# Level products of a gated linear mixer: from zero-padded queries of two heads to one product per head on 64 rows

## The chip, the cores and the metric

The kernel runs on one core of one Trainium2 chip. The metric is device time in microseconds, from launch to end; the profiled execution's span is the time from the first to the last instruction on the core. TensorE's granted clock is reported beside it as a share of its full 2.4 GHz.

## The reference: what is computed

The program is one layer of a hybrid encoder on 2048 tokens of width 1024: a normalization, a projection to 13 groups of columns, four mixers of width 256 each (S5, HGRN2, FoX attention, mLSTM), an output projection, and a SwiGLU feed-forward part, with residuals. All in float32.

The change touches the HGRN2 mixer alone. It has 4 heads of 64 channels. With gates `lf` (logarithms of decays), queries `q`, keys `k` and values `v`, one chunk computes

```
b = cumsum(lf) over time
scores[t, s] = sum over channels of q[t] * k[s] * exp(b[t] - b[s])      for s <= t, else 0
o = (q * exp(b)) @ state + scores @ v
state = exp(b_last) * state + (k * exp(b_last - b))^T @ v
```

The decay is per channel, so `exp(b[t] - b[s])` can't be pulled out of the sum as one factor per time without overflow; it has to be split at a point between s and t.

## The kernel before, in words

The 2048 tokens are handled in four blocks of 512 (`BLK`), each of four chunks of 128 (`P`). The projection of blocks 0 and 1 comes first, then that of blocks 2 and 3, then for each block the output projection and the feed-forward part. `hgrn_mix(c, b)` (L458) runs once per block: for blocks 0 and 1 it is put among the projections as work of high priority (L1660 to L1666), for blocks 2 and 3 it stands in `mixers` (L1626) beside the feed-forward part of the block before. The order in which each engine gets its instructions is not written out by hand. A planner simulates the program with its own costs, places each instruction by priority and by the time at which its operands are ready, and fixes one order per engine; buffers rotate within pools (`tile_pool`), and an instruction that takes a buffer waits for its last readers. So the dense matmuls of the projections (L279, L297) and of the feed-forward part (L1478 gate and up, L1503 down) lie between the mixer's instructions on TensorE.

Channels lie on partitions: a "head pair" p holds 128 rows, head 2p on rows 0 to 63 and head 2p+1 on rows 64 to 127; time lies along the free dimension. For the scores of a chunk, the kernel splits time in seven levels (`LEVELS`, h = 64, 32, ..., 1). At level h each window of 2h times has its keys in its first half and its queries in its second, both decayed towards the window's middle. A level product is one set of matmuls in which all windows of a chunk are done together, and a mask (`c.lvl`) picks the blocks of the result that belong to the level.

For each pair and level the loop at L499 does this:

- GpSimd subtracts the middle's `b` (L509), ScalarE takes two exponentials (L513 for keys, L514 for queries), each 128x256.
- VectorE multiplies the keys into `hK` (L516, 128x256; the halves that hold no keys are zero from a memset at L478) and the queries into `hQ` (L520). `hQ` has the shape 128 x 2 x 256: for each of the two heads a full-height operand in which the rows of the other head stay zero, from the memset at L478. So there are two half-height multiplications, one per head. At level 1 GpSimd copies the queries instead (L526), and the keys are used as they are.
- TensorE does four matmuls (L530), one per chunk: the 128x128 keys of both heads as weights, the padded queries of both heads (2 x 64 columns) as the moving operand. Because of the zeros one product over 128 rows gives both heads' scores side by side, in one PSUM tile from `c.psS` (four buffers, tag `s`, shared with the other mixers and with the transposes of L109).
- VectorE copies the masked blocks into `hA[p]` (L534, `copy_predicated`, 128x512).

After the seven levels of a pair follow the rest of its operands (L535 to L549): decayed queries and keys in place (L541, L542), and the diagonal of each chunk's last time, made with `hL` (L548) and copied into `hA` (L550). After both pairs: transposes of the keys (L567), state updates (L576, L584), outputs from the state and from `hA` (L591, L595), the head-wise normalization and the gate. The gates are loaded into buffers of the tag `hb`, which hold `b` before (L553).

A float32 matmul appears in the trace as two records, each a weight load (PEld) and a matmul (PE); here they are called passes. The dense matmuls work on operands split in two float32r parts, and each of them is one pass.

Of the kernel before, what the change touches and what calls it, by code (L numbers as in the profile page):

```python
# [8 lines left out]
F32 = mybir.dt.float32  # L9
# [3 lines left out]
AF = mybir.ActivationFunctionType  # L13
ALU = mybir.AluOpType
# [4 lines left out]
P = 128  # L19
D = 1024  # L20
KD = D // P
BLK = 512
NEG = -1e30
EPS = 1e-6
LEVELS = (64, 32, 16, 8, 4, 2, 1)
# [153 lines left out]
def l3(t):  # L179
    return t.rearrange("p (c l) -> p c l", l=P)  # L180
# [277 lines left out]
def hgrn_mix(c, b):  # L458
    nc, tc = c.nc, c.tc
    with ExitStack() as ctx:  # L460
        def tp(name, bufs):
            return ctx.enter_context(tc.tile_pool(name=name, bufs=bufs, side=c.side, reuse_waits="tile"))

        p1, p2, ptmp = tp("h_p1", 1), tp("h_p2", 2), tp("h_tmp", 4)

        def ps():
            return c.psS.tile([P, 512], F32, name="ps", tag="s")

        def tmp(name):
            return ptmp.tile([P, BLK], F32, name=name, tag="tmp")  # L470

        nk = 4
        hA = [p1.tile([P, 2, BLK], F32, name=f"hA{p}") for p in range(2)]
        hK = [p1.tile([P, BLK], F32, name=f"hK{p}") for p in range(nk)]
        hQ = [p1.tile([P, 2, 256], F32, name=f"hQ{p}") for p in range(nk)]
        hL = [p1.tile([P, 2, 4], F32, name=f"hL{p}") for p in range(2)]
        for t in (*hA, *hK, *hQ, *hL):
            nc.gpsimd.memset(t, 0.0)  # L478
        v = p1.tile([P, 4, 256], F32, name="hv")
        qs, ks, bs, qes, kds, ebs = [], [], [], [], [], []  # L480
# [9 lines left out]
        for p in range(2):  # L490
            eb = p2.tile([P, 4], F32, name="heb")
            nc.scalar.activation(eb, l3(bs[p])[:, :, P - 1], AF.Exp)
            for h in range(2):
                s = slice(64 * h, 64 * h + 64)
                nc.gpsimd.tensor_copy(hL[p][s, h], l3(qs[p])[s, :, P - 1])
            ebs.append(eb)
        for p in range(2):
            A4 = hA[p].rearrange("p h (c l) -> p h c l", l=P)
            for i, h in enumerate(LEVELS):  # L499
                w = 2 * h  # L500
                nb = BLK // w
                q3 = qs[p].rearrange("p (n w) -> p n w", w=w)
                k3 = ks[p].rearrange("p (n w) -> p n w", w=w)
                Q = hQ[(7 * p + i) % nk]
                if h > 1:
                    b3 = bs[p].rearrange("p (n w) -> p n w", w=w)
                    dd = tmp("hd")
                    d3 = dd.rearrange("p (n w) -> p n w", w=w)
                    nc.gpsimd.tensor_tensor(d3, b3, b3[:, :, h - 1:h].to_broadcast([P, nb, w]), ALU.subtract)  # L509
                    ee = tmp("he")  # L510
                    eq = ee[:, 0:256].rearrange("p (n w) -> p n w", w=h)
                    ek = ee[:, 256:512].rearrange("p (n w) -> p n w", w=h)
                    nc.scalar.activation(ek, d3[:, :, 0:h], AF.Exp, scale=-1.0)  # L513
                    nc.scalar.activation(eq, d3[:, :, h - 1:2 * h - 1], AF.Exp)  # L514
                    K = hK[(7 * p + i) % nk]
                    nc.vector.tensor_tensor(K.rearrange("p (n w) -> p n w", w=w)[:, :, 0:h],  # L516
                                            k3[:, :, 0:h], ek, ALU.mult)
                    for hh in range(2):
                        s = slice(64 * hh, 64 * hh + 64)
                        nc.vector.tensor_tensor(Q[s, hh].rearrange("p (n w) -> p n w", w=h),  # L520
                                                q3[s, :, h - 1:2 * h - 1], eq[s], ALU.mult)
                else:
                    K = ks[p]
                    for hh in range(2):
                        s = slice(64 * hh, 64 * hh + 64)
                        nc.gpsimd.tensor_copy(Q[s, hh].rearrange("p (n w) -> p n w", w=1), q3[s, :, 0:1])  # L526
                pt = ps()
                p3 = pt.rearrange("p (h t) -> p h t", h=2)
                for t in range(4):
                    nc.tensor.matmul(p3[:, :, t * 64:(t + 1) * 64], lhsT=K[:, t * P:(t + 1) * P],  # L530
                                     rhs=Q[:, :, t * 64:(t + 1) * 64], start=True, stop=True)
                av = hA[p].rearrange("p h (n w) -> p h n w", w=w)[:, :, :, h - 1:2 * h - 1]
                mv = c.lvl[:, i].rearrange("p (n w) -> p n w", w=h)[:, None].to_broadcast([P, 2, nb, h])
                nc.vector.copy_predicated(av, mv, pt.rearrange("p (h n w) -> p h n w", h=2, w=h))  # L534
            q, k, bb = qs[p], ks[p], bs[p]  # L535
            b3 = l3(bb)
            e1, e2 = tmp("he1"), tmp("he2")
            nc.gpsimd.tensor_tensor(l3(e2), b3, b3[:, :, P - 1:P].to_broadcast([P, 4, P]), ALU.subtract)
            nc.scalar.activation(e1, bb, AF.Exp)
            nc.scalar.activation(e2, e2, AF.Exp, scale=-1.0)  # L540
            nc.vector.tensor_tensor(q, e1, q, ALU.mult)  # L541
            nc.vector.tensor_tensor(k, e2, k, ALU.mult)  # L542
            qes.append(q)
            kds.append(k)
            pt = ps()
            pl = pt[:, 0:8].rearrange("p (h t) -> p h t", h=2)
            for t in range(4):
                nc.tensor.matmul(pl[:, :, t], lhsT=kds[p][:, t * P:(t + 1) * P], rhs=hL[p][:, :, t],  # L548
                                 start=True, stop=True)  # L549
            nc.vector.tensor_copy(A4[:, :, :, P - 1], pl)  # L550
        gs = []
        for u in range(2):
            g = p2.tile([P, BLK], F32, name="hgs", tag="hb").rearrange("p (t n) -> p t n", t=2)  # L553
# [8 lines left out]
        for u in range(2):  # L562
            pt = ps()
# [7 lines left out]
        for u in range(2):  # L571
            pd = ps()
            for i in range(2):
                for p in range(2):
                    cs = slice((2 * i + p) * P, (2 * i + p + 1) * P)
                    nc.tensor.matmul(pd[:, cs], lhsT=kts[u][:, cs], rhs=v[:, 2 * u + i, p * P:(p + 1) * P],  # L576
                                     start=True, stop=True)
            pd = pd.rearrange("p (i a h d) -> p i a h d", i=2, a=2, h=2)
            for i in range(2):
                t = 2 * u + i  # L580
                for p in range(2):
                    for h in range(2):
                        s = slice(64 * h, 64 * h + 64)
                        nc.vector.scalar_tensor_tensor(S[t + 1][s, p, h], S[t][s, p, h], ebs[p][s, t:t + 1],  # L584
                                                       pd[s, i, p, h], ALU.mult, ALU.add)
            po = ps()
            for i in range(2):
                t = 2 * u + i
                for p in range(2):
                    cs = slice((2 * i + p) * P, (2 * i + p + 1) * P)  # L590
                    nc.tensor.matmul(po[:, cs], lhsT=qes[p][:, t * P:(t + 1) * P],  # L591
                                     rhs=S[t][:, p].rearrange("p h d -> p (h d)"), start=True, stop=False)
                    for h in range(2):
                        c0 = (2 * i + p) * P + h * 64
                        nc.tensor.matmul(po[:, c0:c0 + 64], lhsT=hA[p][:, h, t * P:(t + 1) * P],  # L595
                                         rhs=v[:, t, p * P + h * 64:p * P + h * 64 + 64], start=False, stop=(h == 1))
            nc.scalar.activation(v[:, 2 * u:2 * u + 2], po.rearrange("p (t n) -> p t n", t=2), AF.Copy)
        f = p2.tile([P, 16], F32, name="hf")
# [393 lines left out]
def s5_mats(c, tp, s4q, kt_tile, ps, NCH):  # L992
# [121 lines left out]
    def build(gb, m):  # L1114
# [458 lines left out]
def hybrid_block(ctx, tc, x, w_in, gate_bias, s5_lambda_re, s5_lambda_im, s5_b_re, s5_b_im, s5_c_re,  # L1573
# [52 lines left out]
    def mixers(b):  # L1626
        mlstm_mix(c, b)
        fox_mix(c, b)
        if b + 1 < NB:
            hgrn_mix(c, b + 1)  # L1630
        if b == 1 and c.NHALF > 1:
            s5_mix(c, 1)

    with ExitStack() as s:
# [30 lines left out]
        for h in range(1, c.NHALF):  # L1665
            proj(h, lambda: nullcontext(c.px), {4: [hi(hgrn_mix, 1)], 8: [first]})  # L1666
# [45 lines left out]
```

## Time and profile before

| | |
|---|---|
| three runs | 2840.5, 2851.24, 2850.12 us; median 2850.12 |
| the profiled execution's own time | 2851.47 us |
| its span | 2849.8 us, 40254 instructions |
| granted TensorE clock, mean | 0.982 |
| busy: TensorE (PE), its weight loads (PEld) | 2728.4 us (96%), 2299.9 us (81%) |
| busy: VectorE (DVE), ScalarE (ACT), GpSimd (POOL) | 1654.2, 829.1, 898.5 us |
| moved by DMA | 605 MB |

The busy time of an engine is the union of its instructions' times. A matmul's record is longer than the time for which it keeps the next one waiting, since matmuls are pipelined; what one costs is read from the starts of consecutive ones. The chain of waits follows the end of the program back, at each step to what released the instruction, and gives each engine's share of the span. In a list of instructions, "idle before" is the time that the engine stood idle ahead of it, and the name behind the arrow is what ended that idle time.

### The profile page before, as it was taken

Reading aid. Unit: us, or ns where it says so; the run is one execution under the profiler, and the core shown is the slowest. Engines: PE = TensorE matmul, PEld = TensorE weight load, DVE = VectorE, ACT = ScalarE, POOL = GpSimd, SP = SyncE. Lnnn points to the kernel's source line nnn. Section 1 sums busy time; section 2 is a strip of 40 time slices with the busy share of each in tenths; the row PEclk is TensorE's granted clock in tenths of the full one; section 3 lists DMA queues with packets and bytes.
Section 4 is the critical chain, followed back from the end, with each engine's and each line's share of the span. In section 5 each row is a group of like instructions: output and inputs, shape, how many; then the busy total and the mean of one; then the engine's idle time right before and its main releaser. Section 6 shows DMA issues by size and latency. Waiting matters only on the chain.

```text
span 2849.8 us, 40254 instructions
## 1 busy us (share of the span) xinstructions
PE 2728.4 (96%) x14678; PEld 2299.9 (81%) x14678; DVE 1654.2 (58%) x2795; ACT 829.1 (29%) x1596; POOL 898.5 (32%) x959
## 2 busy tenths in 40 slices
PE   6898989999999999899999999999999999999998
PEld 5797987888887777788787778888877778888886
DVE  7968456575315676875466666645676764522233
ACT  6323325333324333324321233223122332300001
POOL 7554311243215556643210234222022432100001
PEclk9999999999998999999999999999999999999999
DMA  6573594544768977686846656475566556765554
GB/s 200 206 259 130 187 294 152 171 168 159 255 189 280 304 261 253 242 297 233 287 149 218 202 178 226 147 273 207 198 197 196 187 166 222 276 217 189 189 192 140
DMA packets 323108, 605.11 MB, mean 212 GB/s; under 512 B 56160, under 2 KB 146144, under 8 KB 322656
## 3 DMA queue, kind: packets, MB, share of 16 engines
q1 hardware_dynamic: 321888, 602.48, 62.9%
q8 instruction: 116, 1.90, 0.3%
q14 instruction: 80, 0.66, 0.1%
q0 software_dynamic: 1024, 0.07, 0.0%
HBM read 428.42 MB, written 173.35 MB: 211 GB/s over the span
## 4 chain that ended last, share of the span: by engine, by line
PE 66%; DVE 13%; DMA 11%; issue 3%; POOL 2%; SPq 2%; ACT 2%; DVEq 0%; POOLq 0%; ACTq 0%
PE pf L1478 27%; PE pf L1503 14%; PE pf L1395 5%; PE pf L297 5%; PE pf L279 4%; PE ps L913 2%; DMA f_raw<-ka_d 2%; DMA f_raw<-fv_d 1%; DVE hQ L520 1%; DMA f_raw<-kb_d 1%; PE pt L109 1%; DMA b_xt<-in_x_dram 1%; DMA f_raw<-qb_d 1%; DVE hA L534 1%; PE ps L897 1%
## 5 line engine op out<-in xcount | busy, mean ns | idle before, releaser
L1478 PE MATMUL pf<-b_ah,wh 128*128 128x512 f32 (+1 forms) x1536 | 582.2, 379 | 0.0
L1478 PE MATMUL pf<-b_ah,wl 128*128 128x512 f32 (+1 forms) x1536 | 581.7, 379 | 0.0
L1478 PE MATMUL pf<-b_al,wh 128*128 128x512 f32 (+1 forms) x1536 | 580.1, 379 | 0.0
L1503 PE MATMUL pf<-dh,g_h 128*128 128x512 f32 x1408 | 460.7, 396 | 3.6 <-DVE b_acc L1508 3.1
L1478 PEld LDWEIGHTS pf<-b_ah,wl 128*128 128x128 f32 x1536 | 291.8, 190 | 55.0
L1478 PEld LDWEIGHTS pf<-b_ah,wh 128*128 128x128 f32 x1536 | 291.5, 190 | 55.0 <-DVE b_acc L1508 0.6
L1478 PEld LDWEIGHTS pf<-b_al,wh 128*128 128x128 f32 x1536 | 290.6, 190 | 54.6
L1503 PEld LDWEIGHTS pf<-dh,g_h 128*128 128x128 f32 x1408 | 264.8, 189 | 61.9 <-DVE b_acc L1508 5.0
L1503 PE MATMUL pf<-dl,g_h 128*128 128x512 f32 x704 | 276.8, 393 | 0.0
L910 POOL TENSOR_TENSOR f_accs<-f_accs,f_pe 128x512 f32<-128x512 f32 (+3 forms) x144 | 176.8, 1228 | 279.1 <-ACT f_pe L904 276.1
L1508 DVE TENSOR_TENSOR b_acc<-b_acc,pf 128x512 f32<-128x512 f32 x320 | 213.9, 680 | 80.0 <-PE pf L1503 78.5
L90 POOL TENSOR_TENSOR wl<-wr,wh 128x1024 fp32r<-128x1024 f32 (+2 forms) x76 | 189.4, 2495 | 201.7 <-ACT wh L89 195.7
L297 PE MATMUL pf<-wh,aTh 128*128 128x256 f32 (+2 forms) x768 | 220.4, 287 | 2.0 <-ACT stg L323 1.5
L297 PE MATMUL pf<-wl,aTh 128*128 128x256 f32 (+2 forms) x768 | 221.9, 289 | 0.0
L297 PE MATMUL pf<-wh,aTl 128*128 128x256 f32 (+2 forms) x768 | 220.3, 287 | 0.0
L1482 ACT ACTIVATE g_th<-pf 128x512 f32<-128x512 f32 x88 | 52.6, 598 | 392.6 <-PE pf L1478 392.5
L906 DVE TENSOR_TENSOR f_pl<-f_pe,f_ph 128x512 fp32r<-128x512 f32 (+3 forms) x160 | 149.1, 940 | 24.4 <-ACT f_ph L905 18.7
L279 PE MATMUL pf<-aTh,wh 128*128 128x512 f32 (+1 forms) x400 | 159.6, 400 | 1.3 <-ACT hnz L304 1.0
L279 PE MATMUL pf<-aTh,wl 128*128 128x512 f32 (+1 forms) x400 | 158.3, 396 | 0.0
L279 PE MATMUL pf<-aTl,wh 128*128 128x512 f32 (+1 forms) x400 | 157.8, 396 | 0.5 <-DVE aTl L114 0.5
L904 ACT ACTIVATE f_pe<-ps 128x512 f32<-128x512 f32 (+3 forms) x160 | 85.3, 533 | 247.5 <-PE ps L897 103.2
L1483 DVE SCALAR_TENSOR_TENSOR g_th<-g_th,pf 128x512 f32<-128x512 f32 x88 | 60.1, 682 | 163.7 <-ACT g_th L1482 163.5
(520 smaller groups left out, 5165.8 us busy)
## 6 DMA issues: line engine op xcount, KB each, us to landing
dh<-wd_0h SPq DMA_DIRECT2D x66, 256.0 KB
dl<-wd_0l SPq DMA_DIRECT2D x66, 256.0 KB
dh<-wd_1h SPq DMA_DIRECT2D x66, 256.0 KB
dl<-wd_1l SPq DMA_DIRECT2D x66, 256.0 KB
wr<-in_w_ffn_gate_dram SPq DMA_DIRECT2D x22, 512.0 KB
wr<-in_w_ffn_up_dram SPq DMA_DIRECT2D x22, 512.0 KB
dr<-in_w_ffn_down_dram SPq DMA_DIRECT2D x44, 256.0 KB
f_raw<-kb_d SPq DMA_DIRECT2D x80, 132.0 KB
```

The lines of the kernel that those rows point to most:

```text
L90: nc.gpsimd.tensor_tensor(lo, r, f32(hi), ALU.subtract)
L279: nc.tensor.matmul(l3(pt)[:, cut], lhsT=x[k][:, s], rhs=a[:, cut, k], start=(n == 0), stop=(n == 23))
L297: nc.tensor.matmul(pt[:, :w], lhsT=a[:, t, k], rhs=x[k], start=(n == 0), stop=(n == 23))
L904: nc.scalar.activation(pe[:, cs], pt[:, cs], AF.Exp)
L906: nc.vector.tensor_tensor(pl[:, cs], pe[:, cs], f32(ph[:, cs]), ALU.subtract)
L910: nc.gpsimd.tensor_tensor(accs[:, cs], accs[:, cs], pe[:, cs], ALU.add)
L913: nc.tensor.matmul(o, lhsT=w, rhs=r[:, cs], start=(kt + n == 0), stop=(kt + n == NK))
L1395: nc.tensor.matmul(pt, lhsT=a[:, t, k], rhs=w, start=(first and i == 0), stop=(last and i == 2))
L1478: nc.tensor.matmul(l3(pt)[:, s], lhsT=x[:, k], rhs=a[:, s, k], start=(k == 0 and i == 0), stop=(k == KD - 1 and i == 2))
L1483: nc.vector.scalar_tensor_tensor(th, th, 1.0, pts[0], ALU.add, ALU.mult)
L1503: nc.tensor.matmul(pt, lhsT=a[:, s], rhs=w[:, 0], start=(m == 0), stop=(m == 3 * len(fs) - 1))
L1508: nc.vector.tensor_tensor(acc[:, t, ns], acc[:, t, ns], pt, ALU.add)
```

## The change

The queries of both heads of a pair are written in one operation to a 128 x 256 tile without padding (so the zeros of `hQ` are not needed), and each head's product is made by a matmul over its own 64 rows: keys of rows 0 to 63 with queries of rows 0 to 63, and the same for rows 64 to 127, each with 64 moving columns. The results of the two heads go to two PSUM tiles, one per head, each filled by both pairs (256 columns each). So the loops are turned around: level by level, both pairs within a level, and the masked copy is made once per head and level over both pairs. `hA` is held per head instead of per pair, with the pair as its second index; the readers at L550 and L595 are changed to match. The tails of both pairs come after all levels.

```
         nk = 4
-        hA = [p1.tile([P, 2, BLK], F32, name=f"hA{p}") for p in range(2)]
+        hA = [p1.tile([P, 2, BLK], F32, name=f"hA{h}") for h in range(2)]
         hK = [p1.tile([P, BLK], F32, name=f"hK{p}") for p in range(nk)]
-        hQ = [p1.tile([P, 2, 256], F32, name=f"hQ{p}") for p in range(nk)]
+        hQ = [p1.tile([P, 256], F32, name=f"hQ{p}") for p in range(nk)]
-        for t in (*hA, *hK, *hQ, *hL):
+        for t in (*hA, *hK, *hL):
             nc.gpsimd.memset(t, 0.0)
...
+        def operands(p, i, h):
...
+            Q = hQ[(2 * i + p) % nk]
+            if h == 1:
+                nc.gpsimd.tensor_copy(Q.rearrange("p (n w) -> p n w", w=1), q3[:, :, 0:1])
+                return ks[p], Q
...
+            K = hK[(2 * i + p) % nk]
+            nc.vector.tensor_tensor(K.rearrange("p (n w) -> p n w", w=w)[:, :, 0:h], k3[:, :, 0:h], ek, ALU.mult)
+            nc.vector.tensor_tensor(Q.rearrange("p (n w) -> p n w", w=h), q3[:, :, h - 1:2 * h - 1], eq, ALU.mult)
+            return K, Q
+
+        heads = [slice(64 * h, 64 * h + 64) for h in range(2)]
+        for i, h in enumerate(LEVELS):
+            w = 2 * h
+            pts = [ps() for _ in heads]
+            for p in range(2):
+                K, Q = operands(p, i, h)
+                for t in range(4):
+                    for s, pt in zip(heads, pts):
+                        c0 = p * 256 + t * 64
+                        nc.tensor.matmul(pt[:, c0:c0 + 64], lhsT=K[s, t * P:(t + 1) * P], rhs=Q[s, t * 64:(t + 1) * 64],
+                                         start=True, stop=True)
+            mv = c.lvl[:, i].rearrange("p (n w) -> p n w", w=h)[:, None].to_broadcast([P, 2, BLK // w, h])
+            for a, pt in zip(hA, pts):
+                av = a.rearrange("p a (n w) -> p a n w", w=w)[:, :, :, h - 1:2 * h - 1]
+                nc.vector.copy_predicated(av, mv, pt.rearrange("p (a n w) -> p a n w", a=2, w=h))
         for p in range(2):
-            A4 = hA[p].rearrange("p h (c l) -> p h c l", l=P)
-            for i, h in enumerate(LEVELS):
...
-                    for hh in range(2):
-                        s = slice(64 * hh, 64 * hh + 64)
-                        nc.vector.tensor_tensor(Q[s, hh].rearrange("p (n w) -> p n w", w=h),
-                                                q3[s, :, h - 1:2 * h - 1], eq[s], ALU.mult)
...
-                for t in range(4):
-                    nc.tensor.matmul(p3[:, :, t * 64:(t + 1) * 64], lhsT=K[:, t * P:(t + 1) * P],
-                                     rhs=Q[:, :, t * 64:(t + 1) * 64], start=True, stop=True)
...
-                nc.vector.copy_predicated(av, mv, pt.rearrange("p (h n w) -> p h n w", h=2, w=h))
             q, k, bb = qs[p], ks[p], bs[p]
...
-            nc.vector.tensor_copy(A4[:, :, :, P - 1], pl)
+            for h in range(2):
+                nc.vector.tensor_copy(l3(hA[h][:, p])[:, :, P - 1], pl[:, h])
...
-                        nc.tensor.matmul(po[:, c0:c0 + 64], lhsT=hA[p][:, h, t * P:(t + 1) * P],
+                        nc.tensor.matmul(po[:, c0:c0 + 64], lhsT=hA[h][:, p, t * P:(t + 1) * P],
```

## Rows read from the trace of the kernel before

**Rows 1.** Page: TensorE's busy time, and the chain that ended last.
```profile
PE 2728.4 (96%) x14678; PEld 2299.9 (81%) x14678; DVE 1654.2 (58%) x2795; ACT 829.1 (29%) x1596; POOL 898.5 (32%) x959
...
PE 66%; DVE 13%; DMA 11%; issue 3%; POOL 2%; SPq 2%; ACT 2%; DVEq 0%; POOLq 0%; ACTq 0%
```

**Rows 2.** Busy time by stretch, the mixer's four stretches, one dense part.
```profile
core 0: us, PE busy (x) PEld busy (x) DVE busy (x) ACT busy (x) POOL busy (x), PEclk, DMA share, GB/s
200.00:270.00 70.00, 57.64 (x336) 49.30 (x336) 61.56 (x87) 19.97 (x39) 36.44 (x49) 0.98 0.48 164
590.00:660.00 70.00, 65.63 (x380) 57.53 (x379) 58.47 (x96) 21.28 (x49) 32.56 (x50) 0.95 0.42 148
1140.00:1200.00 60.00, 52.67 (x276) 43.27 (x275) 52.95 (x68) 22.29 (x45) 45.85 (x47) 0.97 0.69 243
1758.00:1834.00 76.00, 71.38 (x403) 61.49 (x402) 56.09 (x96) 19.76 (x44) 28.73 (x40) 0.98 0.53 182
sum 276.00, PE 247.32 PEld 211.60 DVE 229.07 ACT 83.29 POOL 143.59; mean PE 61.83 PEld 52.90 DVE 57.27 ACT 20.82 POOL 35.90
...
220.00:240.00 20.00, 17.86 (x97) 14.57 (x96) 19.53 (x30) 6.79 (x16) 9.25 (x14) 1.00 0.29 104
```

**Rows 3.** TensorE's waits: who waited for whom, total us, times, longest us.
```profile
PE ps L530 <- DVE hQ L520: 15.0, 10, 3.5
...
PE ps L548 <- DVE hk L542: 5.9, 4, 2.5
...
PE ps L530 <- DVE hA L550: 4.6, 3, 2.0
...
PE ps L530 <- POOL carry L358: 0.5, 1, 0.5
...
PE ps L530 <- DVE hA L534: 0.4, 1, 0.4
```

**Rows 4.** Instructions by line and form: count, busy us, mean ns, idle before.
```profile
L520 DVE TENSOR_TENSOR hQ<-hq,he 64x256 f32<-64x256 f32 x96 | 60.8, 634 | 1.2 <-POOL hQ L478 0.3
L534 DVE COPY_PREDICATED hA<-lvl,ps 128x512 f32<-128x512 uint8 x56 | 59.3, 1059 | 1.8 <-PE ps L530 0.8
L509 POOL TENSOR_TENSOR hd<-hb 128x512 f32<-128x512 f32 x48 | 56.2, 1177 | 45.7 <-ACT he L514 13.9 <-DVE hq L541 11.0 <-DVE hQ L520 9.7
L530 PE MATMUL ps<-hQ,hK 128*128 128x128 f32 x384 | 55.0, 296 | 20.7 <-DVE hQ L520 15.0 <-DVE hA L550 4.6 <-POOL carry L358 0.5
...
L516 DVE TENSOR_TENSOR hK<-hk,he 128x256 f32<-128x256 f32 x48 | 30.2, 634 | 6.5 <-ACT he L513 5.1 <-POOL hK L478 1.3
...
L526 POOL COPY hQ<-hq 64x256 f32<-64x256 f32 x16 | 8.6, 539 | 1.8 <-PE ps L530 1.3
...
L530 PE MATMUL ps<-hQ,hk 128*128 128x128 f32 x64 | 8.5, 275 | 0.0
...
L478 POOL MEMSET hQ<- 128x512 f32 x16 | 7.7, 523 | 0.0
```

**Rows 5.** Lines L520 and L550: durations in ns, least/median/most.
```profile
L520 DVE TENSOR_TENSOR hQ<-hq,he x96: 395/422/2551, 215.3 to 1806.1; 64x256 f32<-64x256 f32 x96
...
L550 DVE COPY hA<-ps x8: 149/164/172, 252.9 to 1818.6; 128x8 f32<-128x8 f32 x8
```

**Rows 6.** Timeline of TensorE, a burst between dense matmuls: start us, us, instruction.
```profile
1808.03 0.40 PE L1478 MATMUL pf<-b_ah,wh 128*128 128x512 f32 x1
1808.27 1.05 PE L530 MATMUL ps<-hQ,hK 128*128 128x128 f32 x8
1809.08 0.48 PE L1478 MATMUL pf<-b_ah,wl 128*128 128x512 f32 x1
1809.40 0.40 PE L1478 MATMUL pf<-b_al,wh 128*128 128x512 f32 x1
```

**Rows 7.** Timeline of TensorE, passes of 128 and of 64 columns.
```profile
1828.82 0.44 PE L591 MATMUL ps<-hS,hq 128*128 128x128 f32 x2
1829.09 0.56 PE L595 MATMUL ps<-hv,hA 128*128 128x64 f32 x4
1829.48 0.33 PE L591 MATMUL ps<-hS,hq 128*128 128x128 f32 x1
```

**Rows 8.** Timeline of TensorE, matmuls over 4 rows and the next.
```profile
312.19 0.60 PE L690 MATMUL ps<-mwl,selr 4*128 4x4 f32 x4
312.66 0.48 PE L701 MATMUL ps<-mngh,selr 4*128 4x512 f32 x1
312.97 0.39 PE L702 MATMUL ps<-mngl,selr 4*128 4x512 f32 x1
313.29 0.39 PE L703 MATMUL ps<-mask_kq,identb 128*128 128x512 bf16 x1
```

**Rows 9.** The chain that ended last, one piece: start us, us, what.
```profile
1324.06 3.46 PE ps L1321 x16
```

More of the change, by code (lines that the diff above doesn't have):

```diff
@@ L496, in hgrn_mix @@
             ebs.append(eb)
-        for p in range(2):
-            A4 = hA[p].rearrange("p h (c l) -> p h c l", l=P)
-            for i, h in enumerate(LEVELS):
[L500 to L517, printed above, removed]
-                    for hh in range(2):
-                        s = slice(64 * hh, 64 * hh + 64)
-                        nc.vector.tensor_tensor(Q[s, hh].rearrange("p (n w) -> p n w", w=h),
-                                                q3[s, :, h - 1:2 * h - 1], eq[s], ALU.mult)
[L522 to L528, printed above, removed]
-                for t in range(4):
-                    nc.tensor.matmul(p3[:, :, t * 64:(t + 1) * 64], lhsT=K[:, t * P:(t + 1) * P],
-                                     rhs=Q[:, :, t * 64:(t + 1) * 64], start=True, stop=True)
-                av = hA[p].rearrange("p h (n w) -> p h n w", w=w)[:, :, :, h - 1:2 * h - 1]
-                mv = c.lvl[:, i].rearrange("p (n w) -> p n w", w=h)[:, None].to_broadcast([P, 2, nb, h])
-                nc.vector.copy_predicated(av, mv, pt.rearrange("p (h n w) -> p h n w", h=2, w=h))
@@ new lines, in operands @@
+        def operands(p, i, h):
+            w = 2 * h
+            nb = BLK // w
+            q3 = qs[p].rearrange("p (n w) -> p n w", w=w)
+            k3 = ks[p].rearrange("p (n w) -> p n w", w=w)
+            Q = hQ[(2 * i + p) % nk]
+            if h == 1:
+                nc.gpsimd.tensor_copy(Q.rearrange("p (n w) -> p n w", w=1), q3[:, :, 0:1])
+                return ks[p], Q
+            b3 = bs[p].rearrange("p (n w) -> p n w", w=w)
+            dd = tmp("hd")
+            d3 = dd.rearrange("p (n w) -> p n w", w=w)
+            nc.gpsimd.tensor_tensor(d3, b3, b3[:, :, h - 1:h].to_broadcast([P, nb, w]), ALU.subtract)
+            ee = tmp("he")
+            eq = ee[:, 0:256].rearrange("p (n w) -> p n w", w=h)
+            ek = ee[:, 256:512].rearrange("p (n w) -> p n w", w=h)
+            nc.scalar.activation(ek, d3[:, :, 0:h], AF.Exp, scale=-1.0)
+            nc.scalar.activation(eq, d3[:, :, h - 1:2 * h - 1], AF.Exp)
+            K = hK[(2 * i + p) % nk]
+            nc.vector.tensor_tensor(K.rearrange("p (n w) -> p n w", w=w)[:, :, 0:h], k3[:, :, 0:h], ek, ALU.mult)
+            nc.vector.tensor_tensor(Q.rearrange("p (n w) -> p n w", w=h), q3[:, :, h - 1:2 * h - 1], eq, ALU.mult)
+            return K, Q
@@ new lines, in hgrn_mix @@
+        heads = [slice(64 * h, 64 * h + 64) for h in range(2)]
+        for i, h in enumerate(LEVELS):
+            w = 2 * h
+            pts = [ps() for _ in heads]
[10 more added lines that the diff above has]
+                nc.vector.copy_predicated(av, mv, pt.rearrange("p (a n w) -> p a n w", a=2, w=h))
```

## The prediction

> **What bounds the kernel now.** Start with the page's busy shares and its chain of waits [rows 1]. TensorE is busy for 2728.4 of 2849.8 us, and 66% of the chain that ended last is TensorE work against 13% of VectorE. So a microsecond of TensorE time added anywhere moves the end by about a microsecond, unless it falls where TensorE stands idle anyway. That makes two questions: how much TensorE time does the change add or remove, and how much idle time is there for it to fall into.
>
> Next, the table of stretches [rows 2] shows the four places where the linear mixer runs, one for each 512-token block. There the picture is different: VectorE is busy for 229.07 of 276 us, in the dense middle nearly without a gap (19.53 of 20 us from 220 on), and TensorE for 247.32, so 28.7 us of TensorE idle time lies in them (12.4, 4.4, 7.3 and 4.6). The list of TensorE's waits says whose it is [rows 3]: 15.0 us before level products (L530) waiting for the queries that VectorE makes (L520), 4.6 us before them waiting for the copy at L550, 5.9 us before L548 waiting for the decayed keys. Together 25.5 us; with 0.9 us for two smaller ones, 26.4. That is the whole sum that a relieved VectorE can give back.
>
> **Part 1: VectorE and GpSimd work that goes.** The rows by form [rows 4] give prices. The queries are now 96 half-height products of 0.634 us (60.8 us). After, 48 full-height ones remain, of the same shape as L516, which also costs 0.634 us: 30.4 us. So 30.4 us of VectorE go, 7.6 us per stretch (by the median of 0.422 us [rows 5] it would be 20 us in all). On GpSimd the sixteen memsets of hQ go (7.7 us), and the sixteen half copies of level 1 become eight full ones (0.539 us each, so 4.3 us saved). Eight small copies for the last column are added on VectorE (L550 becomes two of half the columns); at the 0.164 us of the present ones [rows 5] they cost 1.3 us, beside other work. The predicated copies (56 of 1.059 us) stay: same number, same 128x512 shape, only their two halves are now two head pairs instead of two heads.
>
> How much of the 26.4 us comes back by that alone? In a stretch no more than its own idle time, and no more than the 7.6 us that VectorE saves: 7.6 + 4.4 + 7.3 + 4.6 = 23.9 us at the very most; none at the least, because the plan is made anew and a wait can settle elsewhere. I take 13 us, a little over half, as VectorE is the engine named in nearly all of these waits.
>
> **Part 2: TensorE work that is added.** Seven levels x two pairs x four blocks x four chunks are 224 products, and the trace has 384 + 64 = 448 records [rows 4]: each float32 product is two passes. The timeline of one burst [rows 6] prices a pass: eight passes start at 1808.27, the second main matmul behind them at 1809.40, and a main matmul alone keeps 0.23 us, so the burst takes 1809.40 - 0.23 - 1808.27 = 0.90 us, 0.112 us a pass. So level products cost 448 x 0.112 = 50.2 us now. The change splits each into one product per head: 448 products, 896 passes, each over 64 rows with 64 moving columns.
>
> Is a pass with 64 columns cheaper than one with 128? Where both follow each other [rows 7], two passes of 128 columns and four of 64 take 1829.48 - 1828.82 = 0.66 us, 0.110 us each. So the columns don't set the pace; loading 128 columns of weights does. Is it cheaper with fewer rows? Four passes with only 4 rows and 4 columns [rows 8] take 312.66 - 312.19 = 0.47 us, 0.117 us each. So neither half the rows nor half the columns makes a pass shorter, as far as passes follow each other in the same rows. What no row shows is two passes in different halves of the array; that is the disputed cost, and I bound it from both sides:
> - Lower end: the two heads load and multiply side by side. A pair then takes 0.112 us, a pass 0.056: 896 x 0.056 = 50.2 us, nothing added.
> - Middle: one after the other, loads hidden as now, 0.112 us each: 100.4 us, 50.2 added.
> - Upper end: one after the other, and the load not hidden behind the pass before it. Small-row passes speak for that [rows 8]: the two 4-row matmuls of 512 columns and the one after them start 0.31 and 0.32 us apart, where full-height ones keep 0.23 [rows 6]. The moving part of a 64-column pass is a quarter of that of a 256-column one, which takes 3.46 / 16 = 0.216 us [rows 9], so 0.054 us; a pass then takes 0.112 + 0.054 = 0.166 us: 148.7 us, 98.5 added.
>
> I take the middle, 50.2 us, since the rows nearest to the new shape (few rows, few columns) cost 0.11 to 0.12 us a pass.
>
> One more cost is bounded by the same timeline [rows 8]: the 128-row matmul that follows the 4-row ones starts 0.32 us after them, 0.09 us later than a plain one. If each of the 56 bursts met that on entry and on leaving, it would be 112 x 0.09 = 10 us. I take nothing, since the 4-row matmul before it is as late with no change of shape, and keep 10 us for the range.
>
> The Trainium skill, TensorEngine Tiling (Array Packing), section Key Properties, says that different tiles can load weights and multiply in parallel, and that a change of tiling mode drains the engine. No row here has two row tiles side by side; by the first half of that rule nothing is added (rival A below gives the time), by the second the 10 us above are.
>
> **Part 3: where the added time falls.** It falls into stretches in which TensorE idles. With 12.5 us more TensorE work per stretch, and VectorE 7.6 us ahead of today, TensorE comes later to each wait and finds it served: nearly all of the 26.4 us are then used up. I take 24 us, not 13, in this case.
>
> **Part 4: what is moved.** The levels of both pairs now come before either pair's tail (L535 to L550). No DMA is added; the loads of q, k, b and v are ahead as before. The gate loads (L554) reuse the buffer of b, which the first pair frees later now, so on SP's queue they, and the weight loads behind them, could stand still; the gates are needed only in the last step of the block, and the plan places them by its own clock, so I cost it at nothing (if that cover went, one weight load late per block, a few us). Two PSUM tiles per level are now held until both pairs are in. One step of a pair costs GpSimd 1.177 us [rows 4], so a buffer is held about that much longer; with four buffers two levels are still under way, as today. Nothing is taken for it.
>
> **The sum.** The profiled execution took 2851.47 us (span 2849.8 and 1.7 around it), 1.35 us over the median of the three runs, 2850.12. 2851.5 + 50.2 - 24 = 2877.7, some 27 us slower than the median. I forecast 2877 us.
>
> **Rivals.**
> *A, the two halves run side by side.* Place: the 8 x 56 products. It decides from the point where a pair of passes takes under about 0.07 us a pass (448 x 0.028 = 12.5 us added, which the idle time swallows). For it: the two heads write different PSUM tiles and alternate. Against it: 4-row passes, which leave most of the array free, run no faster [rows 8]. Added 0, given back 13: 2838 us, and 2828 to 2851 by the ends of part 1. This is the case on the other side.
> *B, side by side, but each half's next load waits for its own pass.* 0.166 / 2 = 0.083 us a pass, 74.4 us, 24.2 added, about 18 given back: 2858 us. For it: the same late starts [rows 8]. The Trainium skill, TensorE: Matmul & The Clock Gate, Part 3 (Packing small matmuls), says that a weight load overlaps a running matmul only where the row groups differ. The full-height passes contradict it (their loads are hidden in the same rows) [rows 6, 7], the 4-row ones fit it [rows 8]; by it this case comes out.
> *C, one after the other with loads in the open.* 98.5 added, 25 given back: 2925 us. Against it: every full-height row hides the load.
> *D, VectorE doesn't get ahead,* because GpSimd's subtraction or the predicated copies set the pace: then 0 instead of 13 given back in A (2851), and little changes in the other cases, as the added work uses the idle time by itself.
>
> The stretches also show the granted clock at 0.95 to 0.98 [rows 2]: about 8 us lost to the lower level (1.2 GHz) after TensorE's idle spells, which belongs to the same gain if they go, and is within the ends above.
>
> **How the numbers follow.** Forecast (about 0.10 to 0.14 us a pass) 0.36, A with D 0.31, B 0.19, C 0.14. What this kernel's measurement can tell from no change is about 0.5%, 14 us: 2836 to 2864. A lies below that for a little over half of its chance (0.17) and within it for the rest; B is within for two thirds (0.13) and above for the rest; the forecast is above nearly always (0.34), C always. Add a little for the plan made anew: faster 0.19, same 0.28, slower 0.53. The range 2834 to 2912 leaves out A's best part and C; the forecast's own range is 2864 to 2900.
>
> **What would show it.** The changed kernel's level products should be 896 records of 64 rows, and the starts in a burst tell the case at once: 16 passes in 0.9 us (A), 1.3 (B), 1.8 (forecast) or 2.7 (C). TensorE's waits for the queries should shrink from 15.0 us to a few, VectorE's query rows should halve to about 30 us, and the hQ memsets should be gone. Starts 0.06 us apart, or waits that do not shrink, would make the prediction wrong.

## The result, and the profile after

The changed kernel takes 2867.58 us (median of five runs, 2865.73 to 2876.61) against 2850.44 for the kernel before: a ratio of 1.0059, 95% interval 1.0041 to 1.0077. It is slower by 17 us. Its profiled execution took 2865.73 us with a span of 2864.0. The forecast of 2877 us had the sign, and the time lies in the range, but the profile shows that it came about in another way.

The table of stretches of the changed kernel, of the places that answer to [rows 2] (columns as there; line numbers behind the mixer are three higher than before):

```profile
200.00:270.00 70.00, 61.61 (x418) 54.88 (x417) 49.58 (x85) 19.64 (x40) 27.84 (x38) 0.76 0.33 111
580.00:650.00 70.00, 65.14 (x495) 60.93 (x493) 46.99 (x90) 19.07 (x46) 27.38 (x38) 0.76 0.32 108
1130.00:1190.00 60.00, 57.34 (x368) 49.40 (x367) 42.87 (x65) 21.38 (x45) 41.91 (x43) 0.78 0.66 226
1750.00:1820.00 70.00, 67.61 (x460) 59.33 (x459) 46.28 (x84) 17.57 (x41) 27.12 (x36) 0.85 0.45 153
```

Look at the column before the last two: TensorE's granted clock is 0.76 to 0.85 where it was 0.95 to 0.98. VectorE, busy for 83% of the four stretches before, is now busy for 69%. The next lines are the level products in the first two stretches, from TensorE's timeline (start us, us, instruction, count, wait before it):

```profile
211.83 2.90 PE L530 MATMUL ps<-hQ,hK 64*128 64x64 f32 x48
216.28 1.11 PE L530 MATMUL ps<-hQ,hK 64*128 64x64 f32 x16 [1.55 <-POOL hL L495]
223.45 2.60 PE L530 MATMUL ps<-hQ,hK 64*128 64x64 f32 x16 [6.06 <-DVE hA L535]
226.25 12.56 PE L530 MATMUL ps<-hQ,hK 64*128 64x64 f32 x112 [0.19 <-DVE hQ L518]
...
596.94 2.00 PE L530 MATMUL ps<-hQ,hK 64*128 64x64 f32 x32
603.80 1.97 PE L530 MATMUL ps<-hQ,hK 64*128 64x64 f32 x16 [4.86 <-DVE hQ L518]
607.28 15.63 PE L530 MATMUL ps<-hQ,hK 64*128 64x64 f32 x144
622.70 4.10 PE L530 MATMUL ps<-hQ,hk 64*128 64x64 f32 x32
```

Here both halves of the story can be read. In the first line 48 passes take 2.90 us; less the 0.27 us of the last one that is 2.63 / 47 = 0.056 us a pass, half of the 0.112 us of a full-height pass [rows 6]. So the two 64-row halves do run side by side, and at full clock 896 passes cost what 448 did. In the fourth line 112 passes take 12.56 us, 0.110 us each: the same pairs at the lower level, 1.2 GHz. And no dense matmul lies between them. In the order that the planner gave TensorE before, the 448 passes form 28 runs of 8 to 32 with dense matmuls in between; after, the 896 form six runs of 48 to 224.

When the clock falls and when it comes back can be read from stretches around the first spell at the lower level in the mixer, which lasts from 218.3 to 252.4 us (the last columns are as above; the count behind TensorE's busy time is its passes):

```profile
218.40:243.60 25.20, 19.37 (x160) 18.63 (x160) 22.34 (x33) 8.58 (x21) 15.85 (x15) 0.50 0.28 91
243.60:252.30 8.70, 8.70 (x28) 7.30 (x27) 6.10 (x10) 1.23 (x2) 0.55 (x2) 0.50 0.08 30
252.50:260.00 7.50, 7.50 (x48) 6.59 (x48) 2.48 (x7) 1.68 (x3) 0.43 (x1) 1.00 0.00 0
```

The clock falls in the wait of 6.06 us that begins at 217.39 us, stays at 0.50 through all 160 level passes that are left, and is back only after 8.7 us of other work. The kernel before has falls in the mixer too, four of them, after stretches in which TensorE waits; there the clock is back after 3.4 to 6.8 us. In the changed kernel four of five such spells last 20 to 34 us, and each of the five ends 4 to 9 us after the last level pass before its end, none with passes running. So the narrow passes need not bring the clock down; it does not come back while they follow one another.

The waits for level products (total us, times, longest us) answer to [rows 3]:

```profile
PE ps L530 <- DVE hQ L518: 8.3, 5, 4.9
PE ps L530 <- DVE hA L535: 8.1, 5, 6.1
```

The wait for the queries fell from 15.0 to 8.3 us, and a new one of 8.1 us stands beside it: products that wait for a PSUM buffer, which VectorE's masked copy (L535) frees. VectorE's query rows answer to [rows 4]:

```profile
L518 DVE TENSOR_TENSOR hQ<-hq,he 128x256 f32<-128x256 f32 x48 | 29.8, 624 | 6.4 <-ACT he L515 5.6 <-DMA s_T<-s_sp 0.7
```

A balance of the whole execution follows from the page alone, for the changed kernel from its span of 2864.0 us, its mean clock and this line:

```profile
PE 2764.2 (97%) x15126; PEld 2336.1 (82%) x15126; DVE 1622.8 (57%) x2755; ACT 833.1 (29%) x1598; POOL 881.3 (31%) x935
```

TensorE's idle time is the span less its busy time; what the clock took is (1 - mean granted clock) x span; the rest is work at full clock. The last column is the time at the lower level in the mixer's four places alone (190 to 290, 570 to 680, 1110 to 1230, 1735 to 1860 us), from the trace's record of the clock. All runs, in us of their profiled executions (clock to three digits, so the loss is good to 1.5 us):

| kernel | span | idle | clock | lost to the clock | rest | at the lower level in the mixer |
|---|---|---|---|---|---|---|
| before | 2849.8 | 121.4 | 0.982 | 51 | 2677 | 17 |
| changed | 2864.0 | 99.8 | 0.968 | 92 | 2672 | 116 |
| 1 old order, 64 rows | 2870.2 | 108.8 | 0.972 | 80 | 2681 | 79 |
| 2 new order, padded | 2869.0 | 132.9 | 0.979 | 60 | 2676 | 44 |
| 3 changed, 128 columns | 2858.9 | 118.3 | 0.980 | 57 | 2683 | 55 |
| 4 changed, heads in turn | 2876.6 | 101.0 | 0.967 | 95 | 2681 | 130 |
| 5 changed, dense between | 2906.9 | 103.9 | 0.963 | 108 | 2695 | 154 |
| 6 old order, 64 rows, 128 columns | 2843.0 | 103.0 | 0.983 | 48 | 2692 | 20 |
| 7 before, half of the queries on GpSimd | 2843.7 | 121.4 | 0.985 | 43 | 2679 | 20 |
| 8 changed, queries in two operations | 2900.8 | 121.2 | 0.962 | 110 | 2669 | 143 |
| 9 as 6, queries on GpSimd | 2847.4 | 107.1 | 0.983 | 48 | 2692 | 17 |
| 10 before, all queries on GpSimd | 2842.7 | 120.7 | 0.981 | 54 | 2668 | 24 |

From before to after, idle time falls by 22 us, the clock takes 41 us more, and the work at full clock is 5 us less. That makes the 14 us between the two profiled executions. Part of the lower level falls into TensorE's idle time, where it costs nothing: 26 us of it after, 17 before. Counted in busy time alone the clock takes 79 us in place of 42, so the difference hardly changes. The clock's record has 187 us at the lower level in all, 102 before.

### The profile page after: what moved, and what is told of

It is laid out like the page before. It is cut to its first block, busy times and chain, and to the rows that moved or that the text cites. A ratio compares the mean times of both kernels' runs of the same rounds, so it can differ in the third digit from the quotient of the medians.

```text
span 2864.0 us, 41103 instructions
## 1 busy us (share of the span) xinstructions
PE 2764.2 (97%) x15126; PEld 2336.1 (82%) x15126; DVE 1622.8 (57%) x2755; ACT 833.1 (29%) x1598; POOL 881.3 (31%) x935
## 4 chain that ended last, share of the span: by engine, by line
PE 55%; DMA 7%; DVE 4%; POOL 1%; issue 1%; ACT 1%; SPq 0%; POOLq 0%; DVEq 0%; ACTq 0%
PE pf L1481 27%; PE pf L1506 15%; PE pf L1398 4%; PE ps L916 2%; DMA f_raw<-kb_d 1%; DMA b_xt<-in_x_dram 1%; DMA f_raw<-ka_d 1%; DMA f_raw<-qb_d 1%; PE ps L900 1%; PE ps L899 1%; PE pt L109 1%; PE ps L530 1%; DMA f_raw<-fv_d 1%; PE ps L841 1%; PE ps L714 0%
## 5 line engine op out<-in xcount | busy, mean ns | idle before, releaser
L1506 PEld LDWEIGHTS pf<-dl,g_h 128*128 128x128 f32 x704 | 133.4, 189 | 27.2
```

The source lines that it names most:

```text
L1506: nc.tensor.matmul(pt, lhsT=a[:, s], rhs=w[:, 0], start=(m == 0), stop=(m == 3 * len(fs) - 1))
```

## The experiments

**1 and 2: the products alone, and the order alone.** Experiment 1 keeps the old order and takes the 64-row products:

```
+                pts = [ps() for _ in range(2)]
                 for t in range(4):
+                    for hh, pt in enumerate(pts):
+                        s = slice(64 * hh, 64 * hh + 64)
+                        nc.tensor.matmul(pt[:, t * 64:(t + 1) * 64], lhsT=K[s, t * P:(t + 1) * P],
+                                         rhs=Q[s, t * 64:(t + 1) * 64], start=True, stop=True)
...
```

> The old order (all levels of one pair, its tail, then the other pair) with the new products on 64 rows: one unpadded query operation, two PSUM tiles per pair and level, two masked copies of 128x256 in place of one of 128x512. Theory 1 (the clock): runs of 64-row passes let TensorE's granted clock fall to 1.2 GHz, so what matters is the products and not the order; the time at the lower level should be near the changed kernel's 187 us (before: 102 us) and the time 2860 to 2875 us. Theory 2 (the order): level by level makes the planner bunch the level products and leaves them waiting; then this one goes back to 2835 to 2852 us with about 100 us at the lower level.

Measured: 2871.63 us, ratio 1.0074 (1.0054 to 1.0094), in the range of theory 1; 160 us at the lower level by the trace's record of the clock. The old order also shows what it costs to put a run of 64-row passes between dense matmuls:

```profile
212.47 0.39 PE L279 MATMUL pf<-aTl,wh 128*128 128x512 f32 x1
212.78 2.00 PE L526 MATMUL ps<-hQ,hK 64*128 64x64 f32 x32
214.72 0.51 PE L279 MATMUL pf<-aTh,wh 128*128 128x512 f32 x1
215.06 0.39 PE L279 MATMUL pf<-aTh,wl 128*128 128x512 f32 x1
```

From the first start to the last are 2.59 us. Two dense matmuls keep 0.23 us each and 32 passes at 0.056 us take 1.79, so 0.34 us are left for entering and leaving the run. The same sum for [rows 6], with eight full-height passes of 0.112 us, leaves 0.01 us. For the 33 runs of this experiment that is some 11 us by estimate.

Experiment 2 swaps the loops of the old body, `for i, h in enumerate(LEVELS): for p in range(2):`, with the tails after them, and keeps the padded queries and 128 rows.

> The new order (level by level, tails last) with the old products over 128 rows and zero-padded queries. Theory 1 (the clock, through the 64-row products): 2845 to 2856 us, about 100 us at the lower clock level, 448 level passes of 0.112 us at full clock. Theory 2 (the order): 2860 to 2875 us and about 185 us at the lower level, as in the changed kernel.

Measured: 2871.44 us, ratio 1.0086 (1.007 to 1.0102), in the range of theory 2, but with 122 us at the lower level, nearer to theory 1. Neither theory alone is right: each part by itself costs about 20 us, and both together no more. The products cost through the clock (80 us lost, against 51) and the entering and leaving of their runs, while idle time falls by 13 us. The order costs through waits: idle time is up 11 us, with 26.8 us before level products for the queries where there were 15.0, and the clock follows with 9 us:

```profile
PE ps L529 <- DVE hQ L519: 26.8, 20, 4.1
PE ps L549 <- DVE hk L543: 9.7, 5, 5.0
```

**3 and 6: more columns, nothing else.** The clock was the suspect; what lets it fall? Experiment 3 moves 128 columns in three of four products (the extra ones are overwritten):

```
                         c0 = p * 256 + t * 64
+                        n = 128 if t < 3 else 64
-                        nc.tensor.matmul(pt[:, c0:c0 + 64], lhsT=K[s, t * P:(t + 1) * P], rhs=Q[s, t * 64:(t + 1) * 64],
+                        nc.tensor.matmul(pt[:, c0:c0 + n], lhsT=K[s, t * P:(t + 1) * P], rhs=Q[s, t * 64:t * 64 + n],
...
```

> The changed kernel, but three of four products move 128 columns in place of 64 (the next chunk's queries too; the extra columns are overwritten by the next product). Theory 1a (the clock falls because too few columns move per pass): two passes side by side are paced by the weight load of about 0.11 us, so 128 columns fit in the same time; the clock stays up, the time at the lower level goes from 187 us back to 100 to 130 us and the time to 2830 to 2850 us. Theory 1b (the clock falls for the 64 rows or for the waits): 180 us or more at the lower level, 2865 to 2880 us. Theory 3 (the passes themselves cost more): slower than the changed kernel, 2875 us or more.

Measured: 2857.54 us, ratio 1.0025 (1.0011 to 1.0038), 118 us at the lower level instead of 187. Theory 1a holds for the clock in the main; the time came 7 us above its range. In the mixer's four places 55 us at the lower level are left of 116, against 17 before. TensorE's order still has seven runs (16 to 224 passes), so it isn't the dense matmuls between them that brought the clock back. And the passes follow each other as fast: 64 of them in 3.79 us, (3.79 - 0.27) / 63 = 0.056 us, in the fourth stretch of experiment 3:

```profile
1773.34 3.79 PE L531 MATMUL ps<-hQ,hK 64*128 64x128 f32 x64
...
1784.68 7.00 PE L531 MATMUL ps<-hQ,hK 64*128 64x128 f32 x64 [0.26 <-DVE hA L536]
```

The clock's return can be seen here too. These are the level passes alone, on both sides of 1790.5 us, where it comes back in the middle of a run:

```profile
1780.40:1790.40 10.00, 8.82 (x73) 8.14 (x72) 0.50 0.16 53
1790.60:1796.00 5.40, 4.02 (x53) 3.39 (x50) 1.00 0.29 82
```

Five of the eight spells of this run in the mixer end like that, with level passes before and behind; in the changed kernel and in experiments 4, 5 and 8, which move 64 columns in the same order, none of 18 does.

What is left are the waits, now 16.5 us for PSUM: with TensorE faster, the masked copies are late. Experiment 6 does the same in the old order, where experiment 1 had only the clock against it (`rhs=Q[s, t * 64:t * 64 + 128]` from a query tile of 320 columns).

> The old order with the products on 64 rows as in the first experiment, but all of them moving 128 columns (queries in a tile of 320 columns, the last 64 of zeros; the extra columns are overwritten or not read). If columns hold the clock up in this order too, the time at the lower level goes from 160 us to 100 to 120 and the time from 2871 to 2845 to 2856 us. If the first experiment's loss is its waits for PSUM (15.6 us) and not the clock, it stays at 2865 us or more.

Measured: 2843.98 us, ratio 0.9973 (0.9961 to 0.9986), a little under the expected range. Against experiment 1 that is 28 us, from the columns: the runs on TensorE are nearly as they were (34 for 33, of 8 to 40 passes), the loss to the clock goes from 80 to 48 us. The wider passes are not quite free: the work at full clock is 11 us more than in experiment 1, and as much more in experiment 3 than in the changed kernel. Against the kernel before, 18 us less of idle time outweigh 15 us more of work, part of which is the entering and leaving of 34 runs. The granted clock in the four stretches from 190, 570, 1120 and 1735 us is the figure after the five busy times, first of experiment 1:

```profile
190.00:290.00 100.00, 90.62 (x614) 78.05 (x614) 71.32 (x119) 30.44 (x61) 44.28 (x52) 0.90 0.46 157
570.00:670.00 100.00, 95.78 (x713) 86.60 (x712) 62.73 (x136) 27.25 (x63) 35.37 (x50) 0.91 0.39 132
1120.00:1220.00 100.00, 94.50 (x543) 77.89 (x542) 59.13 (x102) 29.94 (x61) 56.15 (x54) 0.86 0.64 211
1735.00:1835.00 100.00, 97.83 (x593) 80.49 (x592) 64.44 (x116) 28.38 (x63) 40.43 (x47) 0.93 0.53 177
```

and then of experiment 6:

```profile
190.00:290.00 100.00, 92.52 (x667) 80.86 (x666) 71.16 (x121) 31.10 (x64) 44.39 (x58) 0.95 0.49 164
570.00:670.00 100.00, 94.61 (x703) 83.65 (x702) 68.60 (x141) 28.27 (x65) 34.74 (x56) 0.98 0.40 135
1120.00:1220.00 100.00, 96.59 (x610) 79.89 (x610) 66.59 (x113) 34.16 (x64) 59.88 (x58) 0.97 0.65 223
1735.00:1835.00 100.00, 98.50 (x638) 81.95 (x637) 59.57 (x119) 26.54 (x56) 33.78 (x46) 1.00 0.53 174
```

**4: are the halves really side by side?** The loops over heads and chunks are swapped (`for s, pt in zip(heads, pts): for t in range(4):`), so that four products of the lower rows come before four of the upper.

> The changed kernel, but within a pair and level all four products of the lower 64 rows come first and then the four of the upper 64, so that passes of different halves meet only where the heads change. If the two halves run side by side in the changed kernel (0.06 us a pass at full clock), this takes 0.11 us a pass at full clock and up to 0.22 at the lower one: some 40 us more TensorE time, of which the waits take a part, 2885 to 2910 us. If passes of 64 rows are short by themselves, or if TensorE pairs them over the distance of eight passes, nothing changes: 2865 to 2870 us.

Measured: 2877.22 us, ratio 1.0100 (1.0078 to 1.0122): 10 us over the changed kernel, between the two answers. The first burst shows why:

```profile
212.77 3.61 PE L530 MATMUL ps<-hQ,hK 64*128 64x64 f32 x48
```

(3.61 - 0.27) / 47 = 0.071 us a pass. TensorE still pairs most passes, over a distance of four in program order and not of eight. In the trace's single starts a new run of eight passes begins every 0.50 us, 0.006 us after the fifth pass of the run before, where eight passes one after the other would take 0.90 us. So the last four passes of one half run beside the first four of the other, 0.063 us a pass in the middle of the burst. (A record doesn't name its half; the first pass of a run is known by its longer record, 0.32 us against 0.27.)

**5: dense matmuls between.** If too little work lets the clock fall, full-array work put between should keep it up. Ahead of each set of products:

```
+                for pt in pts:
+                    nc.tensor.matmul(pt[:, p * 256:p * 256 + 256].rearrange("p (c t) -> p c t", c=2), lhsT=c.identr,
+                                     rhs=c.identr[:, None].to_broadcast([P, 2, P]), start=True, stop=True)
```

> The changed kernel with 112 extra matmuls over all 128 rows (identity times identity, 256 columns of float32r, their result overwritten by the level products), one per head, pair and level, ahead of the products that share its PSUM columns. They cost 112 x 0.118 = 13 us of TensorE at full clock and nothing else. Theory 1 (the clock falls in the long runs of 64-row passes because these keep too little of the array at work): the time at the lower level falls from 187 us towards 100 to 130 us, 28 to 43 us come back for 13 paid: 2838 to 2860 us. Theory 1b (the clock falls for the waits, or whatever is in the runs): 180 us or more at the lower level and 2878 us or more.

Measured: 2909.99 us, ratio 1.0215 (1.019 to 1.024). The expectation of theory 1 failed clearly: 219 us at the lower level, more than the changed kernel's 187. The added matmuls ran at the lower level too:

```profile
L528 PE MATMUL ps<-identr 128*128 128x256 f32 x112 | 40.6, 446 | 8.4 <-DVE hA L538 8.2
```

A mean of 446 ns, where dense matmuls of 256 columns elsewhere show 287. So two short dense matmuls per 16 narrow passes do not bring the clock back; they only lengthen the slow spells, now 34 to 41 us each. The work at full clock is up by 23 us, where 13 were expected for the added matmuls; they also cut the passes into 52 runs, and each run has to be entered and left. Why the clock came back in experiments 3 and 6 and not here stays open.

**8: how much is VectorE's relief worth?** The changed kernel with the queries made in two half-height operations again:

```
-            nc.vector.tensor_tensor(Q.rearrange("p (n w) -> p n w", w=h), q3[:, :, h - 1:2 * h - 1], eq, ALU.mult)
+            for s in (slice(0, 64), slice(64, 128)):
+                nc.vector.tensor_tensor(Q[s].rearrange("p (n w) -> p n w", w=h), q3[s, :, h - 1:2 * h - 1], eq[s], ALU.mult)
```

> The changed kernel, but the unpadded queries written by two half-height operations again: VectorE gets its 30 us (20 by the median) back, all else stays. If the relief of VectorE is what gave TensorE's idle time back in the changed kernel (from 98 to 77 us in the profile), the idle time goes up by 10 to 20 us and the time to 2875 to 2890 us. If the idle time fell only because slower level products fill it, 2864 to 2872 us.

Measured: 2903.34 us, ratio 1.0181 (1.0157 to 1.0205), 36 us more than the changed kernel and 13 above the expected range. Idle time is up by 21 us, a little over what was expected, and the clock takes 18 us more, which was not. In this plan, with nothing between the level products, what VectorE lacks is paid twice, as a wait and as clock.

**7, 9 and 10: the relief without the products.** Nothing on TensorE has to change for it. Experiment 7 is the kernel before with `(nc.vector, nc.gpsimd)[hh].tensor_tensor(...)` for the queries.

> The kernel before, with one of the two half-height query operations of each pair and level on GpSimd in place of VectorE: nothing on TensorE changes. VectorE loses 48 x 0.634 = 30 us as in the change, GpSimd gains about 48 x 0.6 = 29 us. If VectorE is what TensorE waits for in the mixer, 5 to 20 us of TensorE's 26 us of waits come back: 2832 to 2847 us. If GpSimd (the subtraction of 1.18 us per step, now with 0.6 more) or the sharing between the two takes its place: 2848 us or more.

Measured: 2837.96 us, ratio 0.9952 (0.9936 to 0.9968), the fastest of all and in the first expected range. TensorE's wait for the queries on VectorE is down to 3.5 us. Its profiled execution, at 2845.39, was the slowest of its eleven runs, so its balance in the table understates the gain.

```profile
PE ps L548 <- DVE hk L542: 9.9, 4, 4.1
PE ps L530 <- DVE hQ L520: 3.5, 4, 1.6
...
L520 POOL TENSOR_TENSOR hQ<-hq,he 64x256 f32<-64x256 f32 x48 | 43.5, 911 | 3.9 <-PE ps L530 0.7
L520 DVE TENSOR_TENSOR hQ<-hq,he 64x256 f32<-64x256 f32 x48 | 42.8, 896 | 0.6 <-POOL hQ L478 0.5
...
L516 DVE TENSOR_TENSOR hK<-hk,he 128x256 f32<-128x256 f32 x48 | 37.3, 782 | 9.3 <-ACT he L513 8.6 <-POOL hK L478 0.7
```

The last three lines say that VectorE was hardly relieved. With GpSimd at work beside it, each of its remaining query products took 0.896 us where one took 0.634 before, and each key product 0.782 where it took 0.634 [rows 4]; VectorE's busy time in all fell from 1654.2 to 1651.5 us. TensorE's idle time is the same 121.4 us as before: what went from the waits for queries came back at other places, 9.9 us before L548 among them. So the time gained is shown, and its cause is not.

Experiment 9 puts the whole query operation of experiment 6 on GpSimd, experiment 10 both halves of the kernel before.

> The sixth experiment's kernel (old order, 64 rows, 128 columns) with the whole query operation on GpSimd instead of VectorE. VectorE loses another 33 us, GpSimd gains about 48 x 0.9 = 43 us. If the two gains (the clock kept up, VectorE relieved) add, 2825 to 2840 us, the best so far. If GpSimd's step (1.14 + 0.9 us) now sets the pace of the levels, TensorE waits for GpSimd by name, and the time is 2842 us or more.

> The kernel before with both half-height query operations on GpSimd: VectorE loses 61 us, GpSimd gains about 96 x 0.9 = 87 us. If VectorE is still what the mixer waits for once half of the queries are gone (the seventh experiment), 2825 to 2838 us. If GpSimd's step of 1.2 + 1.8 us becomes the limit, 2842 us or more, with TensorE waiting for GpSimd's queries.

Measured: 2848.05 us, ratio 0.9992 (0.998 to 1.0004), and 2842.66, ratio 0.9971 (0.996 to 0.9982). The gains of 6 and 7 do not add, and the second half on GpSimd adds nothing to the first one's gain; it may take some of it back, but the two intervals overlap. In neither is GpSimd's query a wait of TensorE of more than a few us (2.8 us in experiment 9, 2.6 in 10), so the reason that was expected, GpSimd's pace, is not shown; the plan is new in each, and that was not taken apart.

## Why the prediction was right in sign, and where it failed

The time fell near the forecast by luck: the forecast added 50 us of passes and took 24 us of idle time off, while the balance shows 41 us of clock, 22 us of idle time and 5 us less work. By its own sign of being wrong (starts 0.06 us apart) the mechanism was wrong.

**The step that failed** is the middle value of part 2: "one after the other, loads hidden as now, 0.112 us each", 50.2 us added. At full clock a pass of the changed kernel takes 0.056 us; rival A's mechanism, given 0.31 with D, is what happened, and the work at full clock did not grow (2677 to 2672). The rows of 4-row passes [rows 8] misled: they follow each other in the same rows and say nothing on passes in different ones. The Trainium skill, TensorEngine Tiling (Array Packing), section Key Properties, had it right that different tiles load and multiply in parallel; 0.056 against 0.112 us agrees.

**What cost the time in its place** is a term that the sum did not have: 41 us lost to the clock. The text counted the clock only as a small gain of about 8 us, since in the trace of before it falls after idle spells. That is so in the changed kernel as well; what it did not ask is whether the clock comes back while passes of half the rows and half the columns run. By chance the lower level brings a pass back to 0.110 us, the very figure of the forecast, so the signature "16 passes in 1.8 us" was met for another reason. Experiments 3 and 6 show that the moved columns are a lever: with 128 columns and still 64 rows the loss is gone in the old order (48 us, 51 before) and mostly gone in the new one (57). Passes of 128 rows and 64 columns were not run, so what the rows add is not shown; and why experiment 5's dense matmuls did not help stays open.

**Part 1** held: the queries take 29.8 us instead of 60.8 (30.4 forecast), the memsets are gone. The 13 us that their relief was to give without added work can be compared with experiments 1 and 6, where the order is the old one and idle time fell by 13 and 18 us. That experiment 7 gains 12.8 us is no measure of it, since VectorE was hardly relieved there. **Part 3**, 24 us of idle time used up, measured 22, but not because TensorE came later: in experiment 8, with the clock's loss even larger and VectorE's queries in two operations again, the idle time is 121.2 us, as in the kernel before.

**Part 4** took nothing for waits on PSUM buffers, and nothing for the new order. Both cost: 8.1 us of waits for the masked copy after and 16.5 in experiment 3, and the order by itself about 20 us in experiment 2 and 14 between experiments 6 and 3. That the buffers are held until both pairs are in is not shown to be the reason, as experiment 1, which does not hold them so, has 15.6 us of the same waits. Rival A's 2838 us failed through the clock: the work did not grow and more idle time was given back than the 13 us it took, but 41 us went to the clock. The switch cost that the prediction kept for the range is real: 0.34 us for each run of 64-row passes between dense matmuls (experiment 1). It is small here, some 2 us by estimate, because the plan has six runs and not the 56 of the prediction's sum.

## What to carry to other kernels

Before a matmul is made smaller, ask what it does to the clock of the work around it: narrow passes can run side by side in no more time and still cost more through the granted clock, and moving more columns than needed, where the columns don't set the pace (0.056 us a pass with 64 and with 128), can be nearly free and bring it back. Where TensorE waits for VectorE, try early to move part of its work to another engine; it touches neither the products nor their order, and here it gained 12.8 us where the restructuring lost 17. But look at what both engines then take: here VectorE's own products became slower, and its busy time hardly fell. A new loop order can take the dense work out from between the small products, so read the planner's new order as a cost of its own.

## What the runs showed of the hardware

- Two float32 passes over 64 rows each, in different halves of the array and with different PSUM tiles, take the time of one full-height pass (0.056 us a pass against 0.112), weight loads included, whether 64 or 128 columns move (changed kernel, experiment 3).
- Such passes do so in part when four products of one half come before four of the other (0.071 us a pass): the first pass of the second half starts beside the fifth of the eight of the first. The Trainium skill, TensorE: Matmul & The Clock Gate, Part 3 (Packing small matmuls), says that a weight load overlaps a running matmul only where the row groups differ; the full array contradicts it: a pass of 128 columns takes 0.112 us [rows 6], and moving them alone takes 0.108 by estimate (half of the 0.216 us for 256 columns, [rows 9]), so the load in the same rows is hidden.
- A run of 64-row passes between full-height matmuls costs 0.34 us beside its passes (experiment 1, at full clock); a run of full-height float32 passes costs 0.01 [rows 6].
- Once the granted clock had fallen to the lower level after a wait, it did not come back, in the new order, during runs of 64-row passes with 64 columns (changed kernel: 0.76 over 70 us; none of 18 spells in four kernels), and with 128 columns it did (experiment 3, five of eight spells). In the old order, with dense matmuls between shorter runs, it came back among passes of 64 columns too (three of nine spells of experiment 1); its four stretches had 0.86 to 0.93 with 64 columns and 0.95 to 1.00 with 128.
- A product of 64x256 on VectorE took 0.896 us on average while GpSimd made the other half (experiment 7), and 0.634 before.
